# A two-layer hybrid trunk: GpSimd's mixer work to VectorE, gates and branches with tokens on the partitions, and a new ordering clock

## The chip, the cores and the metric

One core of one Trainium2 chip runs the whole forward pass. The metric is the device time of one execution in microseconds (us), as the median of several runs. Four compute engines matter: TensorE (PE in the profile; PEld is its weight load), VectorE (DVE), ScalarE (ACT) and GpSimd (POOL). SyncE (SP) issues the weight transfers.

## The reference, cut to what matters

The input has 256 tokens of 1024 features; there are two layers. Each layer is a feed-forward block, a mixer with three branches that share one input projection, and another feed-forward block.

```
x = x + 0.5 * swiglu_ffn(rms_norm(x, ffn1_norm[l]), ...)
h = rms_norm(x, mix_norm[l])
rg_x, rg_g, sb_q, sb_k, sb_v, c_q, c_kv, k_r, gate_logits = split(h @ w_in[l])
u   = causal_depthwise_conv(rg_x, conv_w[l], conv_b[l])        # 4 taps
y_a = rg_lru(u, ...) * gelu(rg_g)                              # linear recurrence over tokens
y_b = stick_breaking_attention(sb_q, sb_k, sb_v)               # 8 heads of 128
y_c = mla_branch(c_q, c_kv, k_r, ...)                          # latent attention, rope, softmax
g_a, g_b, g_c = split(sigmoid(gate_logits))
merged = g_a * (y_a @ w_branch_a) + g_b * (y_b @ w_branch_b) + g_c * (y_c @ w_branch_c)
x = x + merged @ w_out[l]
x = x + 0.5 * swiglu_ffn(rms_norm(x, ffn2_norm[l]), ...)
```

The output is `rms_norm(x, final_norm)`, all in float32.

## The kernel before, in words

**Arithmetic.** A float32 matmul is made of three in the shorter type float32r. A weight piece (128 partitions by 1024 columns) comes by DMA into `raw`; ScalarE rounds it to `hi` and VectorE subtracts, `lo = raw - hi` (`split_to`, lines 414 to 428). Activations are split alike into a tile `r` (`hilo`, line 461). `AHEAD` lets the split of a piece be issued two pieces before TensorE uses it; `hi` and `lo` have four buffers each.

**Two forms of group.** `feature_group` (line 511) makes 256 output features for all tokens: weights are the stationary operand, features lie on the partitions, and per block of 128 by 128 weights it issues one matmul of 512 columns (`hi` against activation high and low parts) and one of 256 (`lo` against the high part). The two column halves of the bank must then be added, by a ScalarE copy and a VectorE addition (`features`, line 580). `token_group` (line 552) makes 512 features for 2 x 128 tokens: activations are stationary, tokens lie on the partitions, and there are three matmuls of 512 columns per block of 128 tokens by 128 inputs. Its result needs no addition.

**Order.** `MIX_ORDER` (line 31) is the order of a mixer's groups, written by hand: `rgx`, `rgg` (recurrent branch), `q`, `k`, `v` (stick-breaking), `cq`, `ckv`, `uq`, `uqr`, `ukv`, `uv` (latent attention), gates `ga`, `gb`, `gc`, branch projections `bra`, `brb`, `brc`, and `out`. Groups of the trunk go into two large PSUM banks `acc`; short ones (`uq`, `ukv`, the last of a stage) into two of four small banks `side`, which the branches' own small matmuls use too. `small_banks` (line 489) makes the program order run ahead with side work until two are free.

**Side work.** Branch chains are generators. Every recorded operation has an estimated cost (class `Op`), and `Clock` keeps a time for each engine. After each weight block `tasks.tick()` issues what `fits` allows (line 266): a side matmul only if its inputs are at most 60 ns late by that clock. All recorded operations carry line 201 in the profile, so they are told apart by tile names. Each engine runs its own list strictly in order.

**GpSimd** has the first tap of the convolution (line 847), two operations of gelu (865, 866), three products of the recurrent chain (910, 925, 934), half of the query rope (1073), and small norm work.

**Gates and branches.** `gate` (line 1243) evacuates, scales by the token norm (a VectorE product) and takes a tanh. `branch` (line 1256) adds the halves, multiplies by the gate and adds to `merged`; the last one splits the sum for `out`.

Of the kernel before, what the change touches and what calls it, by code (L numbers as in the profile page):

```python
# [14 lines left out]
NT = S // 128  # L15
# [16 lines left out]
v0 k0 rgx0 rgx1 k1 q0 q1 cq0 q2 q3 k2 rgx2 v1 k3 rgx3 rgg0 rgg1 rgg2 rgg3  # L32
gb0 uq0 gb1 uq1 gb2 uq2 gb3 uq3 uqr0 brb0 brb1 ckv0 brb2 brb3 ga0 ukv0 ga1 ukv1 uv0 ga2 ukv2
ga3 ukv3 bra0 bra1 uv1 gc0 bra2 gc1 gc2 gc3 brc0 brc1 brc2 brc3 bra3 out0 out1 out2 out3
# [5 lines left out]
    "ga": ("in", C_G, KD), "gb": ("in", C_G + 1024, KD), "gc": ("in", C_G + 2048, KD),  # L40
    "uq": ("uq", 0, 2), "ukv": ("ukv", 0, 2), "bra": ("bra", 0, KD), "brb": ("brb", 0, KD), "brc": ("brc", 0, KD), "out": ("out", 0, KD),
    "dn1": ("dn1", 0, KF), "dn2": ("dn2", 0, KF),
}
TOKENS = {"last": ("dn2", 0, KF), "v": ("in", 4096, KD), "uqr": ("uq", 1024, 2), "uv": ("ukv", 1024, 2)}


def group_stream(what, n):

    if what == "ckv":
        for k in range(0, 9, 3):  # L50
            yield ("ckv0", "in", k, C_C + 256)
            yield ("ckv1", "in", k, C_C + 256)
    elif what in TOKENS:
# [106 lines left out]
class Op:  # L160


    def __init__(self, engine, name, op, args, kw):
        self.f, self.e, self.args, self.kw = getattr(engine, op), name, args, kw
        self.engine = engine
        out = kw.get("out", args[0] if args else None)
        n = 1
        for d in out.shape[1:]:
            n *= d
        outs = [out] + ([kw["accum_out"]] if kw.get("accum_out") is not None else [])  # L170
        aps = [x for x in (*args, *kw.values()) if hasattr(x, "tensor")]
        self.outs = {x.tensor.name for x in outs}
        self.ins = {x.tensor.name for x in aps if all(x is not o for o in outs)}
        self.table, self.tail = None, 80
        if op == "dma_start":
            self.cost, self.tail = 50, 2500
        elif name == "pe":
            self.tail = 165
            wide = op == "matmul" and args[2].dtype == F32
            self.cost = 2.5 + 0.4167 * (4 * n if wide else max(n, 256))  # L180
        elif name == "act":
            self.table = TABLES.get(kw.get("func"))
            extra = sum(90 for k in ("scale", "bias") if not isinstance(kw.get(k, 0.0), (int, float)))
            self.cost = 95 + extra + 0.833 * n
        elif name == "dve":
            fast = op in ("tensor_scalar", "tensor_copy") and all(x.space != bass.MemoryType.PSUM for x in aps)
            rate = {"reciprocal": 6.5, "tensor_tensor_scan": 2.1}.get(op, 0.55 if fast else 1.042)
            self.cost = 68 + rate * n
        else:
            self.cost = 150 + (166 if kw.get("op") == ALU.pow else 2.1) * n  # L190

# [30 lines left out]
class Tasks:  # L222
# [3 lines left out]

    LIMIT = 1800
# [38 lines left out]
    def fits(self, op, t):  # L266
# [4 lines left out]
        if op.e == "pe":  # L271
            if s > c.t["pe"] + 60:
                return False
# [64 lines left out]
def trunk(tc, xT_in, pos_in, w_in, rgw_in, fin_in, const_in, out):  # L338
# [4 lines left out]
    with ctx:  # L343
# [167 lines left out]
        def feature_group(kts, evac, last=0):  # L511
# [19 lines left out]
            return finish(evac, a, tasks.LAST if last else None)  # L531

# [299 lines left out]
        def rg_x(mx, p):  # L832
            def conv(f):
# [5 lines left out]
                for j in range(2):  # L839
# [7 lines left out]
                    gp.tensor_scalar(us, fs, cw(3), vec[:, vo + V_CB + k:vo + V_CB + k + 1], op0=ALU.mult, op1=ALU.add)  # L847
# [12 lines left out]
        def rg_g(mx, p):  # L860
            def gelu(x):
# [17 lines left out]
        def rg_chain(mx, ps):  # L879
# [3 lines left out]
            for p in ps:  # L883
# [26 lines left out]
                gp.tensor_tensor(I, I, u, op=ALU.mult)  # L910
# [14 lines left out]
                gp.tensor_tensor(I, I, T, op=ALU.mult)  # L925
# [8 lines left out]
                gp.tensor_tensor(g, g, T, op=ALU.mult)  # L934
# [127 lines left out]
        def q_rope(mx):  # L1062
# [128 lines left out]
        def mix(nm, ntasks, nxt, l):  # L1191
# [51 lines left out]
            def gate(b, n):  # L1243
                def sigmoid(f):

                    act.activation(out=f, in_=f, func=AF.Tanh, scale=0.5)
                    yield
                    sig[b, n] = f

                def run(a):  # L1250
                    f = yield from scaled(a, mx["nm"], "rb")
                    yield
                    tasks.spawn(sigmoid(f))
                return run

            def branch(i, b, n):

                def run(a):
                    f = yield from FT.take()
                    hl = (yield from RT.take()) if i == 2 else None  # L1260
                    while (b, n) not in sig or (i and n not in merged):
                        yield 1
                    s = sig.pop((b, n))
                    m = merged[n] if i else None
                    for c, ap in parts(a):
                        fc, sc = two(f)[:, c], two(s)[:, c]
                        act.copy(fc, ap[:, :, 256:512])
                        dve.tensor_tensor(fc, ap[:, :, 0:256], fc, op=ALU.add)
                        if type(a) is not list:
                            yield  # L1270
                            give_banks(a)
                        dve.scalar_tensor_tensor(out=fc, in0=sc, scalar=1.0, in1=fc, op0=ALU.add, op1=ALU.mult)
                        if i:
                            mc = two(m)[:, c]
                            dve.tensor_tensor(mc, mc, fc, op=ALU.add)
                        if i == 2:
                            act.copy(hl[:, c, 0], mc)
                            dve.tensor_tensor(hl[:, c, 1], mc, hl[:, c, 0].bitcast(F32), op=ALU.subtract)
                    yield
                    if type(a) is list:  # L1280
                        give_banks(a)
                    FT.give(s)
                    if i == 0:
                        merged[n] = f
                        return
                    FT.give(f)
                    if i == 2:
                        FT.give(m)
                        mT[n] = hl
# [17 lines left out]
            for g in MIX_ORDER:  # L1307
# [21 lines left out]
                elif what in ys:  # L1329
                    mtask[n] = feature_group(Pairs(mx[ys[what]], lambda p: work[what][p:p + 1] if what == "bra" else work[what], KD), branch(turn[g], what[2], n), last=4 if g == branches[-1] else 0)  # L1330
                elif what == "out":
                    out_tasks.append(feature_group(Pairs(mT, lambda p: [mtask[p]], KD), lambda a, n=n: update_x(n, a, 0.5, nxt), last=4 if n == 3 else 0))
                else:
                    feature_group(kts, gate(what[1], n))
                if what in ys and n == 3:
# [182 lines left out]
```

## Time and profile before

| what | us |
|---|---|
| runs of the kernel | 1460.66, 1460.79, 1461.21 (median 1460.79) |
| the profiled execution | 1463.23 |
| its span (first to last instruction) | 1461.4 |
| TensorE busy | 1442.5 (99% of the span) |
| VectorE busy | 1108.8 (76%) |
| ScalarE busy | 888.8 (61%) |
| GpSimd busy | 144.5 (10%) |

A busy share here is the time in which an engine has at least one instruction in flight. Matmuls overlap, so a busy TensorE can still start its matmuls later than its own pace; the timeline's start times show that, the busy share does not. 1.83 us of the profiled execution lie outside its span.

### The profile page before, as it was taken

The page shows a single profiled execution, that of the slowest core. Times are in us where ns is not written, and L with a number is a line of the kernel's source. Part 1 is how long each engine was busy: PE and PEld are TensorE (multiplying, and loading weights), DVE is VectorE, ACT ScalarE, POOL GpSimd, SP SyncE. Part 2 cuts the span into 40 slices and gives each one's busy share as a digit, 9 for nine tenths or more (in the row PEclk, how much of TensorE's full clock was granted, in tenths as well). Part 3 has the DMA queues.
Part 4 walks back from the last instruction along what each step waited for, and adds up shares of the span by engine and source line. Part 5 has one row for each costly group of instructions (what it writes and reads, how often), then busy time and mean ns, then how long its engine had stood idle before and what let it go on. Part 6 is the DMA issues. An engine that isn't in the chain of part 4 may idle for free.

```text
span 1461.4 us, 20833 instructions
## 1 busy us (share of the span) xinstructions
PE 1442.5 (99%) x8276; PEld 1261.0 (86%) x8276; DVE 1108.8 (76%) x1548; ACT 888.8 (61%) x1365; POOL 144.5 (10%) x118
## 2 busy tenths in 40 slices
PE   8999999999999999999999999999999999999998
PEld 7888889888888888888888888898888888888886
DVE  5887567689987788876677776676989877877853
ACT  4665446888665556555455554479885656566543
POOL 2000001123410000000000000111323000100001
PEclk9999999999999999999999999999999999999999
DMA  6555554444543455455545455544444434545452
GB/s 244 201 185 192 200 179 163 170 151 147 197 148 145 171 179 194 179 200 178 198 173 201 177 198 184 200 159 155 141 171 174 173 138 166 199 175 201 176 199 87
DMA packets 37506, 258.17 MB, mean 177 GB/s; under 512 B 4256, under 2 KB 4640, under 8 KB 6816
## 3 DMA queue, kind: packets, MB, share of 16 engines
q1 hardware_dynamic: 35856, 253.16, 48.0%
q0 software_dynamic: 832, 2.62, 0.6%
q8 instruction: 65, 1.06, 0.3%
q10 hardware_dynamic: 720, 1.05, 0.2%
q14 instruction: 33, 0.27, 0.1%
HBM read 255.77 MB, written 1.05 MB: 176 GB/s over the span
## 4 chain that ended last, share of the span: by engine, by line
PE 90%; DVE 7%; issue 1%; ACT 1%; DMA 0%; ACTq 0%; POOLq 0%; POOL 0%; DVEq 0%
PE acc L201 76%; PE side L201 14%; DVE f L201 3%; DVE lo L201 3%; DVE r L201 1%; DMA x<-xT 0%; ACT f L201 0%; ACT hi L201 0%; ACT r L201 0%; ACTq L396 0%; POOLq L1514 0%; POOL rms L201 0%; DVE rms L201 0%; DVEq L201 0%
## 5 line engine op out<-in xcount | busy, mean ns | idle before, releaser
L201 PE MATMUL acc<-r,hi 128*128 128x512 f32 x3116 | 1000.3, 402 | 0.0
L201 DVE TENSOR_TENSOR lo<-raw,hi 128x1024 fp32r<-128x1024 f32 (+1 forms) x478 | 591.4, 1239 | 231.4 <-ACT hi L201 230.2
L201 PEld LDWEIGHTS acc<-r,lo 128*128 128x128 f32 x3116 | 585.2, 188 | 137.7
L201 PE MATMUL acc<-r,lo 128*128 128x256 f32 x3116 | 613.4, 278 | 0.0
L201 ACT CAST hi<-raw 128x1024 fp32r<-128x1024 f32 (+1 forms) x478 | 496.9, 1045 | 128.8 <-PE acc L201 91.9
L201 PEld LDWEIGHTS acc<-r,hi 128*128 128x128 f32 x3116 | 481.5, 189 | 5.0
L201 POOL TENSOR_TENSOR f<-f,f 128x512 f32<-128x512 f32 (+1 forms) x51 | 90.9, 1787 | 1043.3 <-ACT f L201 959.9
L201 ACT COPY f<-acc 128x512 f32<-128x512 f32 x164 | 96.0, 585 | 121.4 <-PE acc L201 121.2
L201 ACT ACTIVATE f<-f 128x256 f32<-128x256 f32 (+3 forms) x190 | 94.9, 502 | 85.6 <-DVE f L201 84.4
L201 DVE TENSOR_TENSOR f<-acc,f 128x512 f32<-128x512 f32 x166 | 113.9, 686 | 41.6 <-ACT f L201 41.2
L201 DVE TENSOR_TENSOR f<-f,f 128x512 f32<-128x512 f32 (+1 forms) x177 | 125.0, 706 | 7.8 <-ACT f L201 1.6
L201 ACT CAST r<-f 128x256 fp32r<-128x256 f32 (+2 forms) x130 | 58.7, 456 | 63.4 <-DVE f L201 59.7
L201 PE MATMUL acc<-hi,r 128*128 128x512 f32 (+2 forms) x344 | 96.9, 358 | 0.0
L201 PE MATMUL side<-r,hi 128*128 128x512 f32 x260 | 84.5, 396 | 0.0
L201 PE MATMUL side<-f,f 128*128 128x256 f32 (+1 forms) x320 | 71.7, 328 | 0.0
L201 PEld LDWEIGHTS acc<-hi,r 128*128 128x128 f32 x344 | 61.6, 189 | 8.3
L201 DVE TENSOR_TENSOR r<-f,r 128x256 fp32r<-128x256 f32 (+2 forms) x130 | 64.7, 502 | 1.9 <-ACT r L201 1.9
L201 PE MATMUL acc<-lo,r 128*128 128x512 f32 (+2 forms) x172 | 61.0, 355 | 0.0
L201 PE MATMUL side<-r,lo 128*128 128x256 f32 x260 | 60.5, 279 | 0.0
L201 PEld LDWEIGHTS side<-r,hi 128*128 128x128 f32 x260 | 45.6, 188 | 7.5
L201 PEld LDWEIGHTS side<-r,lo 128*128 128x128 f32 x260 | 47.0, 188 | 4.0
L201 PEld LDWEIGHTS side<-f,f 128*128 128x128 f32 x320 | 46.0, 191 | 0.5
(95 smaller groups left out, 839.1 us busy)
## 6 DMA issues: line engine op xcount, KB each, us to landing
raw<-w SPq DMA_DIRECT2D x239, 1024.0 KB, 4.8
f<-rgw POOLq DMA_DIRECT2D x8, 256.0 KB, 3.6
raw<-w SPq DMA_DIRECT2D x4, 256.0 KB, 5.7
out<-f SPq DMA_DIRECT2D x4, 256.0 KB, 2.2
x<-xT ACTq DMA_DIRECT2D x3, 256.0 KB, 6.9
f<-fin POOLq DMA_DIRECT2D x2, 256.0 KB, 3.4
cst<-const SPq DMA_DIRECT2D x1, 336.0 KB, 8.3
x<-xT ACTq DMA_DIRECT2D x2, 128.0 KB, 3.8
```

Of the source, the lines that this page charges most:

```text
L201: return self.f(*self.args, **self.kw)
```

## The change

1. **GpSimd to VectorE:** convolution tap, gelu (its two operations become one), the three products of the recurrent chain and the whole query rope.
2. **Tokens on the partitions:** the six groups of gates and of branch projections become token groups of 512 features (`n` is 0 or 1). The gate's norm scale is then one number per partition, which ScalarE applies in the evacuation. A branch multiplies straight out of PSUM. `merged` now has tokens on the partitions, and is turned back by 16 transposes per layer before `out`.
3. **`out0` and `out1`** are computed together (`feature_pair`): both over the first half of `merged`, then both over the second.
4. **The clock:** matmul costs by new formulas, and a side matmul is issued only if its inputs from other engines were written 300 ns (`LATE`) before TensorE's time.
5. **`MIX_ORDER`** is new.

```diff
-v0 k0 rgx0 rgx1 k1 q0 q1 cq0 q2 q3 k2 rgx2 v1 k3 rgx3 rgg0 rgg1 rgg2 rgg3
-gb0 uq0 gb1 uq1 gb2 uq2 gb3 uq3 uqr0 brb0 brb1 ckv0 brb2 brb3 ga0 ukv0 ga1 ukv1 uv0 ga2 ukv2
-ga3 ukv3 bra0 bra1 uv1 gc0 bra2 gc1 gc2 gc3 brc0 brc1 brc2 brc3 bra3 out0 out1 out2 out3
+v0 k0 rgx0 rgx1 k1 q0 q1 cq0 q2 q3 k2 rgx2 v1 k3 rgx3 rgg0 rgg1 uq0 rgg2 uq1 rgg3 uq2
+gb0 uq3 gb1 uqr0 brb0 ckv0 brb1 ukv0 ga0 ukv1 uv0 ga1 ukv2 bra0 ukv3 uv1 gc0 gc1 bra1 brc0 brc1
+outs0 out2 out3
...
-            wide = op == "matmul" and args[2].dtype == F32
-            self.cost = 2.5 + 0.4167 * (4 * n if wide else max(n, 256))
+            self.cost = self.streamed(op, args[2].dtype if op == "matmul" else F32, n)
...
+    def streamed(op, dtype, n):
+        if op == "transpose":
+            return max(109, 0.852 * n)
+        if dtype == F32:
+            return 2 * max(112, 0.852 * n)
+        if dtype == F32R:
+            return 13.5 + 0.4167 * max(n, 256)
+        return 30 + 0.4167 * n
...
-            if s > c.t["pe"] + 60:
+            if s > c.t["pe"] + 60 or op.settled(c) + self.LATE > c.t["pe"]:
                 return False
...
-                gp.tensor_scalar(t, t, 0.044715, 1.0, op0=ALU.mult, op1=ALU.add)
-                gp.tensor_tensor(t, t, x, op=ALU.mult)
-                act.activation(out=t, in_=t, func=AF.Tanh, scale=0.7978845608028654)
+                dve.scalar_tensor_tensor(out=t, in0=t, scalar=1.0 / 0.044715, in1=x, op0=ALU.add, op1=ALU.mult)
+                act.activation(out=t, in_=t, func=AF.Tanh, scale=0.7978845608028654 * 0.044715)
...
-                gp.tensor_tensor(I, I, u, op=ALU.mult)
+                dve.tensor_tensor(I, I, u, op=ALU.mult)
...
-                    rope((gp, dve)[t], split_heads(f, 8), split_heads(qs[t], 8), split_heads(tmp, 8), 8, t)
+                    rope(dve, split_heads(f, 8), split_heads(qs[t], 8), split_heads(tmp, 8), 8, t)
...
             def gate(b, n):
...
-                    f = yield from scaled(a, mx["nm"], "rb")
+                    fs = []
+                    for t in range(NT):
+                        f = yield from FT.take()
+                        act.activation(out=f, in_=bank_of(a, t), func=AF.Copy, scale=mx["rcol"][t])
+                        fs.append(f)
...
             def branch(i, b, n):
...
+                    for t, f in enumerate(fs):
+                        dve.scalar_tensor_tensor(out=f, in0=f, scalar=1.0, in1=bank_of(a, t), op0=ALU.add, op1=ALU.mult)
+                        if i:
+                            dve.tensor_tensor(merged[n][t], merged[n][t], f, op=ALU.add)
...
+                        for q in range(2):
+                            x = yield from transpose_pair(merged[n], q * 256)
+                            hl = yield from RT.take()
+                            hilo(x, hl)
```

**How the order moves.** Three places are shown. The first is TensorE in the change, at the end of group `rgg1` (bank `acc1`) and the start of `uq0` (banks `side3` and `side0`). The rows between belong to a pair of stick-breaking heads: `tri_r` is the cumulative sum over keys, `f24` and `f21` are the attention weights.

```order
L222 MATMUL acc1_85<-r2_92,hi_2816 128x512 x2
L222 MATMUL acc1_85<-r2_92,lo_2817 128x256 x2
L222 MATMUL side3_89<-r11_101,tri_r_75 128x384 x2
L222 MATMUL side3_89<-f5_111,cst_72 128x128
L222 MATMUL side0_86<-r10_100,tri_r_75 128x384 x2
L222 MATMUL side0_86<-f7_113,cst_72 128x128
L222 MATMUL side1_87<-f24_130,f12_118 128x256
L222 MATMUL side1_87<-f24_130,f13_119 128x128
L222 MATMUL side1_87<-f21_127,f12_118 128x256
L222 MATMUL side1_87<-f21_127,f13_119 128x128
L222 MATMUL side3_89<-r12_102,hi_2864 128x512
```

In the kernel before, `uq0` came after `rgg3` and `gb0`, where no such pair was open; there its first rows stand among matmuls of the recurrent chain:

```order
L201 MATMUL acc0_84<-r2_92,hi_2979 128x512 x2
L201 MATMUL acc0_84<-r2_92,lo_2980 128x256 x2
L201 MATMUL side1_87<-r3_93,r13_103 128x256 x4
L201 MATMUL side0_86<-r11_101,hi_3029 128x512
L201 MATMUL side3_89<-r11_101,hi_3029 128x512
L201 MATMUL side0_86<-r11_101,lo_3030 128x256
L201 MATMUL side3_89<-r11_101,lo_3030 128x256
```

So in the change eight side matmuls of one pair stand together between two groups, where before one row of side work stood. The second place is VectorE in the change at the same point of the program, and then ScalarE. `f28` and `f19` are the evacuations of `rgg0` and `rgg1`, `f7` and `r10` lead to the second `tri_r` above, `r8` is the pair's split output.

```order
L222 TENSOR_TENSOR lo_2888<-raw_2703,hi_2887 128x1024
L222 TENSOR_TENSOR f19_125<-acc1_85,f19_125 128x512
L222 TENSOR_TENSOR f19_125<-f19_125,f2_108 128x512
L222 SCALAR_TENSOR_TENSOR f7_113<-side0_86,f21_127 128x384
L222 TENSOR_TENSOR r10_100<-f7_113,r10_100 128x384
L222 TENSOR_TENSOR r8_98<-side1_87,r8_98 128x2x256
L222 TENSOR_TENSOR lo_2933<-raw_2775,hi_2932 128x1024
L222 TENSOR_TENSOR f4_110<-side3_89,f4_110 128x256
```

On VectorE the addition `f19` and one of the recurrent chain (`f2`) stand ahead of the pair's `f7`, `r10` and `r8`. ScalarE in the change, at the same point of the program:

```order
L222 COPY f19_125<-acc1_85 128x512
L222 ACTIVATE f27_133<-f28_134 128x512
L222 CAST r10_100<-f7_113 128x384
L222 ACTIVATE f24_130<-side3_89 128x384
L222 ACTIVATE f21_127<-side0_86 128x384
L222 CAST r8_98<-side1_87 128x2x256
L222 CAST hi_2932<-raw_2775 128x1024
```

On both engines the rows that lead to `r10` stand behind the evacuation `f19` of `rgg1`. The third place is TensorE in the change inside `outs0`: the transposes of the second half of `merged` (`f24`, `f21` here) and the first matmuls on their split, `r8`.

```order
L222 MATMUL acc1_85<-r14_104,hi_4395 128x512 x2
L222 MATMUL acc1_85<-r14_104,lo_4396 128x256 x2
L222 MATMUL side0_86<-cst_72,f21_127 128x128
L222 MATMUL side0_86<-cst_72,f24_130 128x128
L222 MATMUL side0_86<-cst_72,f21_127 128x128
L222 MATMUL side1_87<-cst_72,f24_130 128x128
L222 MATMUL side1_87<-cst_72,f21_127 128x128
L222 MATMUL side1_87<-cst_72,f24_130 128x128
L222 MATMUL side1_87<-cst_72,f21_127 128x128
L222 MATMUL acc0_84<-r8_98,hi_4432 128x512 x2
```

Seven transposes stand directly ahead of the matmuls that read their result; before, `out0` had none there.

## Rows read from the trace of the kernel before

**Rows 1.** The page's first part: busy time and share of the span, by engine.
```profile
PE 1442.5 (99%) x8276; PEld 1261.0 (86%) x8276; DVE 1108.8 (76%) x1548; ACT 888.8 (61%) x1365; POOL 144.5 (10%) x118
```

**Rows 2.** Windows, one stretch of the first mixer: us, busy us of each engine, clock, DMA.
```profile
320.00:411.00 91.00, 87.46 (x516) 77.12 (x515) 85.32 (x114) 67.62 (x110) 35.75 (x26) 1.00 0.46 162
```

**Rows 3.** Timeline of TensorE, up projection: start us, us, what; feature groups.
```profile
99.87 0.62 PE L201 MATMUL acc<-r,hi 128*128 128x512 f32 x2
...
110.32 0.63 PE L201 MATMUL acc<-r,hi 128*128 128x512 f32 x2
```

**Rows 4.** Timeline of TensorE, a token group (`v0`).
```profile
199.23 0.39 PE L201 MATMUL acc<-lo,r 128*128 128x512 f32 x1
...
205.35 0.39 PE L201 MATMUL acc<-lo,r 128*128 128x512 f32 x1
```

**Rows 5.** Timeline of TensorE: three of a set of four transposes, and the next matmul.
```profile
395.17 0.55 PE L201 MATMUL side<-cst,f 128*128 128x128 f32 x3 [0.16 <-DVE f L201]
395.48 0.70 PE L201 MATMUL acc<-r,hi 128*128 128x512 f32 x2
```

**Rows 6.** Timeline of TensorE in the first mixer, recurrent branch; in brackets idle time, releaser.
```profile
335.23 0.36 PE L201 MATMUL side<-r,r 128*128 128x256 f32 x1
336.47 0.39 PE L201 MATMUL side<-r,r 128*128 128x256 f32 x1 [0.88 <-DVE r L201]
338.57 0.28 PE L201 MATMUL side<-r,r 128*128 128x256 f32 x1
340.31 0.62 PE L201 MATMUL side<-r,r 128*128 128x256 f32 x3 [1.46 <-DVE r L201]
```

**Rows 7.** Timeline of TensorE in the first mixer, latent of keys and values.
```profile
402.29 0.40 PE L201 MATMUL acc<-r,lo 128*128 128x256 f32 x2
403.73 0.70 PE L201 MATMUL side<-f,cst 128*128 128x256 f32 x2 [1.04 <-DVE f L201]
```

**Rows 8.** Groups by line and form: count, busy us, mean ns, idle before.
```profile
L201 ACT COPY f<-acc 128x512 f32<-128x512 f32 x164 | 96.0, 585 | 121.4 <-PE acc L201 121.2
L201 DVE TENSOR_TENSOR f<-acc,f 128x512 f32<-128x512 f32 x166 | 113.9, 686 | 41.6 <-ACT f L201 41.2
L201 DVE TENSOR_TENSOR f<-f,f 128x512 f32<-128x512 f32 x169 | 121.6, 720 | 7.7 <-ACT f L201 1.6
L201 DVE SCALAR_TENSOR_TENSOR f<-side,f 128x384 f32<-128x384 f32 x16 | 8.7, 547 | 0.0
L201 ACT CAST r<-f 128x384 fp32r<-128x384 f32 x16 | 8.0, 513 | 1.4 <-DVE f L201 1.4
L201 DVE TENSOR_TENSOR r<-f,r 128x384 fp32r<-128x384 f32 x16 | 9.5, 602 | 0.0
L201 ACT ACTIVATE f<-side 128x384 f32<-128x384 f32 x32 | 15.7, 490 | 8.6 <-PE side L201 8.0
L201 ACT CAST r<-side 128x512 fp32r<-128x512 f32 x16 | 9.4, 586 | 17.3 <-PE side L201 17.2
L201 DVE TENSOR_TENSOR r<-side,r 128x512 fp32r<-128x512 f32 x16 | 10.9, 683 | 5.1 <-ACT r L201 5.1
```

**Rows 9.** Timeline of ScalarE in the first mixer.
```profile
325.58 0.51 ACT L201 CAST r<-f 128x384 fp32r<-128x384 f32 x1 [0.71 <-DVE f L201]
326.11 1.28 ACT L136 ACT_TABLE_LOAD   x1
327.40 0.64 ACT L201 ACTIVATE f<-f 128x512 f32<-128x512 f32 x1
327.94 1.04 ACT L201 CAST hi<-raw 128x1024 fp32r<-128x1024 f32 x1
```

**Rows 10.** VectorE's `lo`, first in 743 to 903, then in 320 to 411: ns min/median/max.
```profile
L201 DVE TENSOR_TENSOR lo<-raw,hi x58: 1215/1224/1227, 744.7 to 900.2; 128x1024 fp32r<-128x1024 f32 x58
L201 DVE TENSOR_TENSOR lo<-raw,hi x29: 1207/1224/2332, 322.3 to 410.1; 128x1024 fp32r<-128x1024 f32 x29
```

More of the change, by code (lines that the diff above doesn't have):

```diff
@@ L52, in group_stream @@
             yield ("ckv1", "in", k, C_C + 256)
+    elif what == "outs":
+        for h in range(2):
+            for n in range(2):
+                for k in range(KD // 2 * h, KD // 2 * (h + 1), 2):
+                    yield ("two", "out", k, 256 * n)
     elif what in TOKENS:
@@ L190, in __init__, with settled @@
             self.cost = 150 + (166 if kw.get("op") == ALU.pow else 2.1) * n
+    @staticmethod
+    def streamed(op, dtype, n):
[6 more added lines that the diff above has]
+        return 30 + 0.4167 * n
+    def settled(self, c):
+        return max((c.written[n][0] for n in self.ins if n in c.written and c.written[n][1] != self.e), default=0.0)
     def when(self, c, after=0.0):
@@ L222 @@
 class Tasks:
+    LATE = 300
     LIMIT = 1800
@@ L531, in feature_group, with feature_pair @@
             return finish(evac, a, tasks.LAST if last else None)
+        def feature_pair(kts, evacs):
+            nk = len(kts)
+            a = [bank() for _ in range(2)]
+            it = iter(kts)
+            for f in range(2):
+                half = [next(it) for _ in range(nk // 2)]
+                for n in range(2):
+                    for i, (h, _, hl) in enumerate(half, f * nk // 2):
+                        if i % 2 == 0:
+                            wh, wl = next_sub()
+                        cs_ = [slice((i % 2) * 256 + b * 128, (i % 2) * 256 + (b + 1) * 128) for b in range(2)]
+                        for b, c in enumerate(cs_):
+                            pe.matmul(a[n][:, b], wh[:, c], hl, start=i == 0, stop=False, skip_group_check=True)
+                        for b, c in enumerate(cs_):
+                            pe.matmul(a[n][:, b, 0:256], wl[:, c], h, start=False, stop=i == nk - 1, skip_group_check=True)
+                        tasks.tick()
+            return [finish(e, x) for e, x in zip(evacs, a)]
         def plain_group(c, xg, evac, norm):
@@ L1258, in run @@
                 def run(a):
-                    f = yield from FT.take()
-                    hl = (yield from RT.take()) if i == 2 else None
                     while (b, n) not in sig or (i and n not in merged):
                         yield 1
[L1263 to L1269, printed above, removed]
-                            yield
[L1271 to L1278, printed above, removed]
@@ new lines, in run @@
+                    yield
+                    give_banks(a)
+                    if i == 0:
+                        merged[n] = fs
+                        return
+                    FT.give(*fs)
+                    if i == 2:
+                        for q in range(2):
+                            x = yield from transpose_pair(merged[n], q * 256)
+                            hl = yield from RT.take()
+                            hilo(x, hl)
+                            yield
+                            side.give(x)
+                            mT[2 * n + q] = hl
+                        FT.give(*merged[n])
@@ L1329, in mix @@
                 elif what in ys:
-                    mtask[n] = feature_group(Pairs(mx[ys[what]], lambda p: work[what][p:p + 1] if what == "bra" else work[what], KD), branch(turn[g], what[2], n), last=4 if g == branches[-1] else 0)
+                    mtask[n] = token_group(Pairs(mx[ys[what]], lambda p: work[what][p:p + 1] if what == "bra" else work[what], KD), branch(turn[g], what[2], n), last=4 if g == branches[-1] else 0)
+                elif what == "outs":
+                    out_tasks += feature_pair(Pairs(mT, lambda p: [mtask[p // 2]], KD), [lambda a, n=n: update_x(n, a, 0.5, nxt) for n in range(2)])
                 elif what == "out":
-                    out_tasks.append(feature_group(Pairs(mT, lambda p: [mtask[p]], KD), lambda a, n=n: update_x(n, a, 0.5, nxt), last=4 if n == 3 else 0))
+                    out_tasks.append(feature_group(Pairs(mT, lambda p: [mtask[p // 2]], KD), lambda a, n=n: update_x(n, a, 0.5, nxt), last=4 if n == 3 else 0))
                 else:
-                    feature_group(kts, gate(what[1], n))
-                if what in ys and n == 3:
+                    token_group(kts, gate(what[1], n))
+                if what in ys and n == 1:
                     RT.give(*mx[ys[what]].values())
```

36 lines of the change are left out of this document (15 added, 21 removed).

## Prediction, made before the change was run

> **What bounds the kernel now.** I read the busy table first: TensorE is busy for 1442.5 of the 1461.4 us of the span, VectorE for 1108.8, ScalarE for 888.8, GpSimd for 144.5 [rows 1]. Work taken from the other three engines is therefore worth something only where TensorE waits for them. The table by windows shows the densest stretch of the first mixer: from 320 to 411 us VectorE is busy for 85.32 of 91 us and TensorE for 87.46, at a granted clock of 1.00 [rows 2]. There VectorE could matter. A busy share does not show a late start, because matmuls overlap, so I read the starts in the timeline. A pair of a feature group's matmuls (512 and 256 columns) takes (110.32 - 99.87) / 30 = 0.348 us [rows 3]; three matmuls of 512 columns in a token group take 3 x (205.35 - 199.23) / 27 = 0.68 us [rows 4]. Against such paces I looked for starts that come late. In a mixer three stand out: two `r` products of the recurrent chain, where 1.24 and 1.74 us lie between two starts whose pace is 0.12 us, so 1.12 and 1.62 us are lost, both released by VectorE [rows 6]; and the latent of keys and values, where 1.44 us lie between two starts whose pace is 0.23, so 1.21 us are lost [rows 7]. That is 3.95 us per layer. The rest of TensorE's time is its own work, so what counts is the number of its matmuls, and the waits that the new order makes.
>
> **The change part by part.**
>
> *Tokens on the partitions.* Twelve matrices of 1024 by 1024 (three gates and three branches in two layers) change their form. As features, one is 64 pairs, 64 x 0.348 = 22.29 us [rows 3]. As tokens, it is 96 matmuls of 512 columns at 0.2267, 21.76 us [rows 4]. Twelve times the difference is -6.3 us. The order counts bear this out: 1536 feature matmuls fewer, 1152 token matmuls more. Added are 32 transposes of `merged`, each a start apart from the next by (395.48 - 395.17) / 3 = 0.103 us [rows 5], together +3.3 us. **Net -3.0 us.**
>
> *Evacuations.* 46 ScalarE copies of 585 ns and 46 VectorE additions of 686 ns go [rows 8]; 24 scaled ScalarE evacuations and 24 VectorE products out of PSUM come. TensorE does not wait for any of these before, so I cost the difference at nothing. The cover is TensorE's own work; without it the engines would still be lighter.
>
> *GpSimd's work on VectorE.* Thirty-two products of 128 by 512 leave GpSimd, with 8 other steps of gelu, 16 conv taps and 12 rope operations. On VectorE the form f<-f,f rises only from 169 to 171 instructions, because the gates' and branches' products leave it; in all VectorE goes from 1550 to 1530. GpSimd's load falls from 123 to 55. VectorE's weight differences `lo` have the same median beside GpSimd work as without (1224 ns), but there the longest took 2332 ns against 1227 [rows 10]; TensorE was not late for `lo` anywhere before, so I count nothing for this. The chain whose `r` was late by 1.12 and 1.62 us [rows 6] is shorter by GpSimd's hand-overs, and the margin of 300 ns asks for inputs that are written. I take both waits, and that of [rows 7], as **gone: -3.95 x 2 = -7.9 us**.
>
> *`uq0` between `rgg1` and `rgg2`.* `small_banks` makes the program issue side work until two small banks are free. In the changed order that pulls eight side matmuls of a stick-breaking pair in between, and on ScalarE and VectorE their inputs stand behind the evacuation of `rgg1`. From the end of `rgg1` the chain is, by the groups' means: copy 0.585, addition 0.686, then about 0.6 of the following `f2` product before the next starts (0.72 for its whole), `f7` 0.547, `r10` on ScalarE 0.513 and on VectorE 0.602 [rows 8]; then the sum over keys on TensorE with some 0.5, the exponential 0.490 [rows 8] and the product with the values, some 0.35; both are estimates from 384 and 3 x 256 columns at the pace of [rows 4]. Together about 5.4 us with hand-overs. TensorE has about 1.6 us of work of its own beside it (eight side matmuls). **+3.8 us per layer.** The ends: 3.0 if the chain starts with `f2` overlapped and hand-overs cost nothing, 4.5 if each step pays another 0.1 us, which is what ScalarE's overlap of consecutive operations shows [rows 9].
>
> *`outs0`.* Seven transposes stand directly ahead of the matmuls on their split. From the last one a ScalarE rounding of 586 ns and a VectorE difference of 683 ns [rows 8] and about 0.4 us of hand-overs, 1.7 us, lie before the next matmul that needs both; 0.55 us of that is covered by transposes. **+1.1 us per layer**, between 0.5 and 1.5.
>
> *Other small banks.* Three later places in the new order ask for a small bank or an input within a microsecond of its last reader: `uq2` (0.45), the latent ahead of `ukv0` (0.6) and `uv1` behind the evacuation of `bra0` (0.8). The trace of before has no such row; between nothing and 1.85 us per layer I take the middle, **+0.9**.
>
> *Sum.* -3.0 - 7.9 + 2 x (3.8 + 1.1 + 0.9) = +0.7 us. On the profiled execution, 1463.23, that is 1463.9. The median of the runs is 1460.79, and 2.4 us lower; by the same difference the changed kernel's median is **1461.5**. About 0.2% (2.9 us) is what a measurement can tell from no change, so I forecast no difference. With the bounds of the new waits alone this case runs from 1457 to 1465.
>
> **The rivals.**
>
> *Faster: the new waits are small.* If the chain behind `rgg1` takes its low end of 3.0, and the other small banks are free in time, the sum is -10.9 + 2 x (3.0 + 1.1) = -2.7; with `outs0` covered as well it is -4.9, that is 1455.9. For it speaks that the margin of 300 ns and 68 fewer GpSimd operations make the rest of the side work arrive earlier, and that the trace before has few late starts outside [rows 6, 7]. Against it, the rows behind `f19` are in strict order on both engines, and no margin applies where `small_banks` forces the issue.
>
> *Slower: ScalarE's weight roundings come late.* Between `rgg0` and `gb1` the change's order has nine table loads on ScalarE where the stretch of [rows 2] had four. One takes 1.28 us [rows 9], so five more are 6.4 us on an engine that was busy for 67.62 of 91 us [rows 2]. Its idle time is mostly waiting for a side bank in order, and so can't all be used. Weights are rounded two pieces ahead, and a piece of eight blocks lasts 8 x 0.348 = 2.8 us [rows 3], so TensorE loses time once a lead of 5.6 us is used up. Then between 0.8 us (6.4 less 5.6) and all of 6.4 us per layer is lost: 3.6 us in the middle, and 1461.5 + 7.2 = 1468.7. It decides from the point where `hi` is the last input of a weight matmul to arrive. Against it: in the window ScalarE had 23.4 us idle, and the feature evacuations of gates in that stretch are replaced by fewer operations.
>
> Here a rule and a row differ. The next activation starts 1.29 us after the load does, and the one before it ends as the load starts: nothing is lost around it [rows 9]. The Trainium skill, "ScalarE: Activation LUTs", section "What ACT_TABLE_LOAD costs", gives about 1283 ns for the load and some 1380 ns for a drain, 2.66 us for each switch of set. The load agrees with the trace, the drain doesn't. By that rule (an estimate from that page) five more loads would cost 13.3 us per layer, 7.7 beyond the lead, and the kernel would take about 1477 us. Since the row shows no such drain, I give that case 2 in 100.
>
> *Slower: the change doesn't remove the waits.* The recurrent chain keeps its length on the two other engines, and VectorE now does all of it. If the waits of [rows 6, 7] only move to other rows, 7.9 us come back: 1461.5 + 7.9 = 1469.4. For it: VectorE is busy for 85.32 of 91 us there [rows 2], and GpSimd's 35.75 us are of work that in part goes to it. Against it: at the new place the chain runs beside weight matmuls until the margin is met.
>
> **How the numbers follow.** I give my forecast 0.42, the faster rival 0.28, late roundings 0.17, waits that move 0.11 and the table loads' drain 0.02. The predicted time is the likeliest, 1461.5. The range reaches from a little below the faster rival's 1455.9 (the low end of `outs0`, 2 x 0.6, and rounding) to just past 1469.4: 1454 to 1470. Faster by over 0.2% is below 1457.9, 0.28; within it 0.42; slower, above 1463.7, 0.30.
>
> **What would show it.** In the changed profile, TensorE's timeline should show a stretch of about 5 us between `rgg1`'s last matmul and `uq0`'s first, with idle time released by ScalarE and VectorE in turn; a start about 1 us late at the first matmul on `r` in `out0`; and no row like those of [rows 6, 7]. Starts of token groups in gates and branches should be 0.227 us apart, and 384 matmuls be missing. The faster rival shows a stretch of 4.5 us or less behind `rgg1`; late roundings show as starts of `acc<-hi,r` matmuls released by ScalarE's `hi` between `rgg0` and `gb1`; waits that move as `side<-r,r` rows with over 1 us idle, released by VectorE. I would be wrong altogether if TensorE's pace in token groups of gates were not that of `v0`, by 12 x 96 x 0.01 = 11.5 us for each 0.01 us.

## The result, and the profile after

The changed kernel takes 1475.22 us (median of 4 runs, 1474.57 to 1475.75), the one before 1461.0 us on the same chip: ratio 1.0096, interval 1.0078 to 1.0113. The kernel is slower by 14 us where no difference was forecast, and lies outside the range of 1454 to 1470.

The first part of its page answers to [rows 1]. TensorE's busy time hardly grows, and every other engine is less busy: VectorE by 47.7 us, ScalarE by 11.2, GpSimd by 101.

```profile
PE 1447.9 (98%) x7924; PEld 1247.4 (85%) x7924; DVE 1061.1 (72%) x1528; ACT 877.6 (60%) x1341; POOL 43.4 (3%) x50
```

A first answer comes from the starts of the same weight piece in both timelines of TensorE: from its first matmul in `v0` to a first matmul in the next feed-forward block. I call that stretch a **mixer** below; it leaves out what happens at the start of the program, and in most kernels here the two mixers differ by 0.2 us or less. Before, the mixers last 566.29 - 203.77 = 362.52 us and 362.68; in the change, 570.79 - 201.44 = 369.35 and 369.27. That is twice 6.7 us, 13.4 of the 14.2 us lost. The feed-forward blocks last the same to within 0.1 us. (The two profiled executions differ by only 11.0 us, since the one before reached its first split weight piece 2.3 us later, at 25.1 us of its span against 22.8.)

The place is the first one of the prediction. TensorE in the change at the end of `rgg1` and the start of `uq0`, in the timeline:

```profile
323.02 0.40 PE L222 MATMUL acc<-r,lo 128*128 128x256 f32 x2
323.25 0.51 PE L222 MATMUL side<-r,tri_r 128*128 128x384 f32 x2
323.60 0.38 PE L222 MATMUL side<-f,cst 128*128 128x128 f32 x2
327.46 1.28 PE L222 MATMUL side<-r,tri_r 128*128 128x384 f32 x2 [3.49 <-ACT r L222]
328.55 0.63 PE L222 MATMUL side<-f,cst 128*128 128x128 f32 x2
328.97 2.44 PE L222 MATMUL side<-f,f 128*128 128x256 f32 x8
331.16 0.71 PE L222 MATMUL side<-r,hi 128*128 128x512 f32 x2
```

The reader sees 7.9 us between the first side matmul (323.25) and `uq0` (331.16), for the eight rows of side work of the order above, which are 16 instructions in the trace. From 323.71 (the last start before the stop; its row groups two) to 327.46 TensorE starts nothing. The chain that it waits for, on ScalarE and then on VectorE:

```profile
323.62 0.58 ACT L222 COPY f<-acc 128x512 f32<-128x512 f32 x1
324.10 0.64 ACT L222 ACTIVATE f<-f 128x512 f32<-128x512 f32 x1
326.90 0.51 ACT L222 CAST r<-f 128x384 fp32r<-128x384 f32 x1 [2.17 <-DVE f L222]
```
```profile
323.86 1.22 DVE L222 TENSOR_TENSOR lo<-raw,hi 128x1024 fp32r<-128x1024 f32 x1
324.99 0.68 DVE L222 TENSOR_TENSOR f<-acc,f 128x512 f32<-128x512 f32 x1
325.71 0.69 DVE L222 TENSOR_TENSOR f<-f,f 128x512 f32<-128x512 f32 x1
326.32 0.55 DVE L222 SCALAR_TENSOR_TENSOR f<-side,f 128x384 f32<-128x384 f32 x1
327.44 0.56 DVE L222 TENSOR_TENSOR r<-f,r 128x384 fp32r<-128x384 f32 x1 [0.58 <-ACT r L222]
```

It is the chain of the prediction, row by row: copy, a weight difference that keeps VectorE until 325.0, addition, product `f2`, `f7`, `r10`. What the prediction does not have stands in the table by windows of the change, in the column after POOL's, the granted clock:

```profile
324.00:327.00 3.00, 0.00 (x0) 0.00 (x0) 2.83 (x4) 0.83 (x3) 0.00 (x0) 1.00 0.25 49
327.00:331.00 4.00, 3.54 (x10) 2.94 (x11) 0.56 (x1) 1.29 (x3) 0.00 (x0) 0.57 0.53 225
331.00:334.00 3.00, 3.00 (x19) 2.62 (x18) 1.68 (x2) 2.56 (x5) 0.00 (x0) 1.00 0.02 5
```

After the stop the clock falls to 0.57 in the mean of four microseconds (0.50 is the lower of its two levels, 1.2 GHz), and the side matmuls that `uq0` waits for run slowly: eight of them take 2.44 us, against 1.72 at a clock of 1.00 in e6 below.

Five more late starts of TensorE in the first mixer of the change, in order: at `uq2`, at the latent of [rows 7], at `ukv0`, at `uv1`, and behind the transposes of `outs0`:

```profile
346.90 0.47 PE L222 MATMUL side<-r,hi 128*128 128x512 f32 x1 [0.24 <-DVE f L222]
...
402.88 0.70 PE L222 MATMUL side<-f,cst 128*128 128x256 f32 x2 [1.64 <-DVE f L222]
...
407.80 0.50 PE L222 MATMUL side<-r,hi 128*128 128x512 f32 x1 [0.22 <-ACT f L222]
...
457.10 0.50 PE L222 MATMUL side<-hi,r 128*128 128x512 f32 x1 [0.49 <-DVE r L222]
...
535.66 0.72 PE L222 MATMUL acc<-r,hi 128*128 128x512 f32 x2 [0.96 <-DVE r L222]
```

Against the usual pace these starts are late by 0.40, 1.80, 0.46, 0.84 and 1.21 us. The late `r` products of [rows 6] are gone.

### The profile page after: what moved, and what is told of

Read it like the earlier page. It is cut to its first block, busy times and chain, and to the rows that moved or that the text cites. A ratio compares the mean times of both kernels' runs of the same rounds, so it can differ in the third digit from the quotient of the medians.

```text
span 1472.4 us, 19989 instructions
## 1 busy us (share of the span) xinstructions
PE 1447.9 (98%) x7924; PEld 1247.4 (85%) x7924; DVE 1061.1 (72%) x1528; ACT 877.6 (60%) x1341; POOL 43.4 (3%) x50
## 3 DMA queue, kind: packets, MB, share of 16 engines
q10 hardware_dynamic: 720, 1.05, 0.2%
HBM read 255.77 MB, written 1.05 MB: 174 GB/s over the span
## 4 chain that ended last, share of the span: by engine, by line
PE 83%; ACT 9%; DVE 5%; issue 2%; DMA 0%; POOL 0%; POOLq 0%; SPq 0%; ACTq 0%
PE acc L222 69%; PE side L222 14%; ACT f L222 4%; DVE f L222 3%; ACT hi L222 2%; ACT L143 2%; DVE lo L222 1%; DVE r L222 1%; ACT r L222 1%; DMA raw<-w 0%; POOL rc L222 0%; POOLq L1554 0%; POOL rms L222 0%; SPq L419 0%; DVE rms L222 0%
## 5 line engine op out<-in xcount | busy, mean ns | idle before, releaser
L222 PE MATMUL acc<-r,hi 128*128 128x512 f32 x2380 | 756.1, 399 | 1.9 <-DVE r L222 1.9
L222 PEld LDWEIGHTS acc<-r,lo 128*128 128x128 f32 x2380 | 447.1, 188 | 105.5
L222 PE MATMUL acc<-r,lo 128*128 128x256 f32 x2380 | 468.0, 278 | 0.0
L222 PEld LDWEIGHTS acc<-r,hi 128*128 128x128 f32 x2380 | 364.5, 189 | 4.4 <-DVE r L222 2.8
L222 PE MATMUL acc<-hi,r 128*128 128x512 f32 (+2 forms) x1048 | 341.7, 392 | 0.0
L222 PEld LDWEIGHTS acc<-hi,r 128*128 128x128 f32 x1048 | 194.3, 188 | 35.1
L222 PE MATMUL acc<-lo,r 128*128 128x512 f32 (+2 forms) x524 | 198.5, 379 | 0.0
L222 PEld LDWEIGHTS acc<-lo,r 128*128 128x128 f32 x524 | 98.7, 188 | 16.3
L222 DVE TENSOR_TENSOR f<-acc,f 128x512 f32<-128x512 f32 x120 | 82.1, 685 | 16.5 <-ACT f L222 16.4
L222 PE MATMUL side<-hi,r 128*128 128x512 f32 x200 | 64.4, 394 | 1.0 <-DVE r L222 1.0
```

Source lines behind the costliest of these rows:

```text
L222: return self.f(*self.args, **self.kw)
```

## The experiments

All times are against the kernel before on the same chip. The mixer durations are worked out from each trace as above.

| kernel | median us | ratio to before, interval | mixers, us |
|---|---|---|---|
| before | 1461 to 1463 | | 362.5, 362.7 |
| the change | 1475.22 | 1.0096, 1.0078 to 1.0113 | 369.4, 369.3 |
| e1 uq0 behind rgg3 | 1458.74 | 0.9976, 0.9967 to 0.9986 | 361.5, 361.5 |
| e2 stop half filled | 1475.34 | 1.0084, 1.0070 to 1.0098 | 368.3, 369.4 |
| e3 no margin | 1476.09 | 1.0094, 1.0080 to 1.0108 | 369.3, 369.3 |
| e4 GpSimd's work back | 1474.95 | 1.0082, 1.0070 to 1.0095 | 369.6, 370.2 |
| e5 e1 and e4 | 1475.87 | 1.0098, 1.0084 to 1.0111 | 369.4, 370.1 |
| e6 stop filled | 1471.89 (one run) | | 368.3, 368.3 |
| e7 e1, old clock | 1473.30 | 1.0080, 1.0067 to 1.0092 | 368.8, 369.0 |
| e8 before with part 1 | 1472.09 | 1.0073, 1.0061 to 1.0086 | 368.7, 368.7 |
| e9 uq0 in a large bank | 1464.73 | 1.0019, 1.0010 to 1.0029 | 365.0, 365.0 |
| e10 e1, uv1 later | 1460.20 | 0.9991, 0.9982 to 1.0000 | 362.0, 362.0 |
| e11 e1, no margin | 1460.47 (one run) | | 361.4, 361.4 |
| e12 e5, old clock | 1469.31 | 1.0051, 1.0037 to 1.0065 | 366.7, 366.7 |

**e1: `uq0` behind `rgg3`.**

```diff
-rgg0 rgg1 uq0 rgg2 uq1 rgg3 uq2
-gb0 uq3 gb1 uqr0 brb0 ckv0 ...
+rgg0 rgg1 rgg2 rgg3 uq0
+gb0 uq1 gb1 uq2 brb0 uq3 uqr0 ckv0 ...
```

The groups `uq1` to `uq3` and `uqr0` move back with it.

> Edit: uq0 stands after rgg3 instead of between rgg1 and rgg2 (uq1, uq2, uq3 one place later each), all else as in the changed kernel. Theory (the loss is the stop behind rgg1: 3.65 us of late start and then some 2 us of half clock, per layer): both go, 2 x 5.7 = 11.4 us, so 1475.2 - 11.4 = 1463.8, give or take 2; no window at a clock under 1.00 in the mixer. Rival (VectorE's or ScalarE's load is the cause, the place only shows it): the wait moves to another row and the time stays within 3 us of 1475.2.

The kernel becomes faster than both. Its timeline of TensorE shows the two `tri_r` pairs of the same pair of heads apart, each between weight matmuls, and none of them late; the clock in the window that was low is 1.00:

```profile
327.89 0.51 PE L222 MATMUL side<-r,tri_r 128*128 128x384 f32 x2
...
328.37 0.71 PE L222 MATMUL acc<-r,hi 128*128 128x512 f32 x2
...
329.86 0.52 PE L222 MATMUL side<-r,tri_r 128*128 128x384 f32 x2
```
```profile
327.00:331.00 4.00, 4.00 (x26) 3.65 (x25) 4.00 (x8) 3.68 (x7) 0.00 (x0) 1.00 0.70 244
```

A mixer loses 7.8 us, not 5.7: in the same step the late start at the latent of keys and values (1.80 us in the change) went, and the two small ones at `uq2` and `ukv0` (0.40 and 0.46). With the 3.65 and 0.42 us of the two `r10` starts and 1.05 us for the clock (e6) that makes 7.8. Moving a group deals the order of what follows anew. The theory holds, its price was low by 2 us per layer.

**e2 and e6: the stop filled with work.** In `stick_pair`, for the pair that stands in the stop:

```diff
+                if p == 3 and j == 1:
+                    o = yield from side.take()
+                    for i in range(FILL):
+                        pe.matmul(o[:, 0:128], warm, warm, start=True, stop=True)
```

The ordering clock counts these matmuls at nothing, so that all other work keeps its order.

> Edit: 30 small bf16 matmuls on zeros (128 columns) into the pair's still unused output bank, at the place of the stop behind rgg1, in both layers; the order of all other instructions stays. It adds work that is thrown away. Theory (the granted clock falls because TensorE stands still for 3.5 us): the chain on ScalarE and VectorE is as long as before, but TensorE is busy and the clock stays at 1.00 from 327 to 331 us, so 2 x about 2.1 us come back: 1471. Rival (the slow matmuls after the stop have another cause, their operands or banks): 1475.2 or a little more, the clock low as before.

> Edit: 58 instead of 30 small matmuls in the stop behind rgg1; 30 of them took 1.84 us and left 1.82 us of idle time. Theory (the clock falls because TensorE has nothing to do for some microseconds): with the stop filled to within 0.2 us the clock is 1.00 in both layers, and each mixer lasts about 1.1 us less than the 369.3 of the changed kernel, 368.2. Rival: the clock falls in at least one layer as before.

With 30 matmuls the fill lasted 1.84 us, and 1.82 us of idle time stayed behind it. In the first layer the clock held, in the second it fell, though the instructions are the same. The windows of e2, first layer, then second:

```profile
328.00:330.00 2.00, 0.66 (x2) 0.41 (x3) 1.15 (x3) 0.90 (x2) 0.00 (x0) 1.00 0.83 307
330.00:332.00 2.00, 2.00 (x12) 1.72 (x12) 0.00 (x0) 0.49 (x1) 0.00 (x0) 1.00 0.43 180
...
1054.00:1056.00 2.00, 0.71 (x2) 0.31 (x2) 1.24 (x3) 0.90 (x2) 0.00 (x0) 0.86 0.78 274
1056.00:1058.00 2.00, 2.00 (x7) 1.82 (x8) 0.00 (x0) 0.49 (x1) 0.00 (x0) 0.50 0.51 213
```

The first mixer was shorter by 1.1 us, the second was not; so e2 alone was inconclusive. With 58 matmuls (e6) the clock is 1.00 in both layers and both mixers are shorter by 1.0 us than in the change. TensorE in e6:

```profile
322.62 0.51 PE L223 MATMUL side<-r,tri_r 128*128 128x384 f32 x2
...
323.18 3.40 PE L223 MATMUL side<-warm 128*128 128x128 bf16 x58
326.85 0.44 PE L223 MATMUL side<-r,tri_r 128*128 128x384 f32 x1 [0.26 <-ACT r L223]
327.44 0.44 PE L223 MATMUL side<-r,tri_r 128*128 128x384 f32 x1 [0.15 <-DVE r L223]
...
327.94 1.72 PE L223 MATMUL side<-f,f 128*128 128x256 f32 x8
329.42 0.71 PE L223 MATMUL side<-r,hi 128*128 128x512 f32 x2
```

So the fall of the clock is a consequence of the standstill, and costs about 1.05 us per layer (1.10 and 0.96); I had put it at 2.1. The standstill itself is not shortened by any filling: the chain on the other engines is as long as before.

**e3 and e11: no margin.**

```diff
-            if s > c.t["pe"] + 60 or op.settled(c) + self.LATE > c.t["pe"]:
+            if s > c.t["pe"] + 60:
```

> Edit: the margin of 300 ns is taken out of the rule (60 ns late is allowed again), new matmul durations kept. Theory: the margin has no part in the loss; the stop behind rgg1 is forced by the banks and stands: 1475 within 2 us. Rival (the margin makes side work late and so the small new waits): 3 to 6 us faster, about 1470, with the stop still there.

> Edit: uq0 behind rgg3, new matmul costs, margin of 300 ns taken out. Theory (of the new clock, the costs moved the stop and the margin does nothing): mixers as with uq0 moved alone, 361.5 within 0.3 us. Rival (the margin did it): a stop at uq0 as with the old clock, mixers near 368.9.

The margin changes nothing that can be seen: 369.3 with and without it in the change, 361.4 and 361.5 with `uq0` moved.

**e4 and e5: GpSimd's work back on GpSimd**, in the change and with `uq0` moved. The diff is that of part 1, turned round.

> Edit: GpSimd's work goes back to GpSimd (tap, gelu, three products, half of the rope), all else as in the changed kernel. Theory (this part of the change only removed the two waits of the recurrent chain): those waits come back in part and the stop behind rgg1 stays: 1475 to 1481. Rival (the load on VectorE makes the chain behind rgg1 long): the stop shrinks by the f2 product and more, and the kernel is 3 us or more faster than 1475.2.

> Edit: uq0 behind rgg3 as in the run before, and GpSimd's work back on GpSimd. Theory (moving that work to VectorE is by itself a gain, since it removes late r products of the recurrent chain; the loss was the place of uq0): 2 to 4 us per layer slower than with uq0 moved alone, 1463 to 1467, with starts of r products late by 1 us and more, released by products that follow GpSimd. Rival (VectorE's load is what hurts): as fast or faster than 1458.7.

In e4 the stop behind `rgg1` is gone: `uq0` starts directly behind it. So part 1 did take part in it, which my theory had denied. But other waits come in its place, one of them of the kind of [rows 6], and the sum is 0.3 to 1.0 us per layer worse. In e4 and e5, the latest rows of TensorE are:

```profile
354.82 0.50 PE L222 MATMUL side<-r,r 128*128 128x256 f32 x2 [2.38 <-DVE r L222]
```
```profile
332.75 0.44 PE L222 MATMUL side<-r,tri_r 128*128 128x384 f32 x1 [1.98 <-DVE r L222]
...
393.30 0.33 PE L222 MATMUL side<-cst,f 128*128 128x128 f32 x1 [2.13 <-POOL f L222]
```

e5 against e1 is what part 1 is worth where the order suits it: 7.9 and 8.6 us per mixer, against 2 to 4 expected. Nor did the loss come by the late `r` products that I had named: none is late in e5; a sum over keys waits for VectorE, with the clock at 0.50 behind it, and transposes wait for GpSimd. The rival, that VectorE's load is what hurts, falls for e5; for e4 both were half right.

**e7 and e12: the old clock**, with `uq0` moved, and the same with GpSimd's work back.

```diff
-            self.cost = self.streamed(op, args[2].dtype if op == "matmul" else F32, n)
+            wide = op == "matmul" and args[2].dtype == F32
+            self.cost = 2.5 + 0.4167 * (4 * n if wide else max(n, 256))
```

(and the margin out, as in e3)

> Edit: uq0 behind rgg3, and the old clock (old matmul costs, no margin). Theory (the clock's new numbers make issue times truer, and are a small gain or none once the order is right): within 3 us of 1458.7, rather above. Rival (the clock is what put the waits at the latents, 0.6 and 0.3 us per layer, and others): 2 us or more faster than 1458.7.

> Edit: token groups, transposes, out0 with out1 and uq0 behind rgg3; GpSimd's work on GpSimd, old clock: the change's parts 2 and 3 without 1 and 4. Theory (each part deals the order anew, and a stop comes where a demand for two small banks meets an open pair): with nothing tuned to it, waits of 5 us and more per layer, mixers of 365 to 371. Rival (the token form itself is the gain, the others don't matter): own work 1.5 us per layer less than before and the old waits, mixers near 361 to 363.

I expected e7 within 3 us of e1; its mixers are 7.3 and 7.5 us longer. Its trace shows the very stop of the change, now at the place to which `uq0` had been moved:

```profile
336.71 1.28 PE L223 MATMUL side<-r,tri_r 128*128 128x384 f32 x2 [3.23 <-ACT r L223]
337.79 0.63 PE L223 MATMUL side<-f,cst 128*128 128x128 f32 x2
338.21 2.53 PE L223 MATMUL side<-f,f 128*128 128x256 f32 x8
340.49 0.71 PE L223 MATMUL side<-r,hi 128*128 128x512 f32 x2
```

Since e11 shows that the margin does nothing, it is the matmul costs. That by the old ones the pair's second half was held back until `uq0` demanded the banks is my reading of the order of the rows, not tried by itself. In e12 there is no such stop, but the two waits of the kernel before stand there again, to the same length as [rows 6], and, in the first layer, four of 0.8 to 1.9 us at the latents, `uv1` and `outs0`. The mixers, 366.7 us, lie where the theory put them, but by these waits and not by a stop:

```profile
334.41 0.39 PE L223 MATMUL side<-r,r 128*128 128x256 f32 x1 [0.88 <-DVE r L223]
...
338.25 0.63 PE L223 MATMUL side<-r,r 128*128 128x256 f32 x3 [1.45 <-DVE r L223]
```

**e8: part 1 alone in the kernel before** (the diff of part 1).

> Edit: the kernel before with part 1 of the change alone (GpSimd's work on VectorE). Theory: the two late r products (1.12 and 1.62 us per layer) go, the rest stays: 1461 - 5.5 = 1455.5. Rival (VectorE, busy for 94% of the stretch from 320 to 411 us, becomes the bound): waits of the same size or larger in that stretch, 1461 or slower.

The rival's outcome, by two mechanisms. The late `r` products of [rows 6] are gone, as I expected, and the wait of [rows 7] as well. In their place a stop of the same kind stands ahead of `uq0`, which in that kernel follows `gb0`: the two `tri_r` starts are late by 0.7 and 1.7 us, and the clock falls behind them. Windows of e8:

```profile
342.00:344.00 2.00, 0.57 (x2) 0.32 (x3) 1.66 (x3) 0.22 (x1) 0.00 (x0) 1.00 0.96 393
344.00:346.00 2.00, 2.00 (x9) 1.73 (x9) 0.00 (x0) 0.49 (x1) 0.00 (x0) 0.55 0.18 74
...
444.00:446.00 2.00, 0.00 (x0) 0.00 (x0) 1.89 (x6) 1.66 (x5) 0.00 (x0) 1.00 0.00 0
446.00:448.00 2.00, 1.78 (x7) 1.65 (x8) 1.39 (x2) 0.37 (x1) 0.00 (x0) 0.65 0.03 8
```

At this stop the load on VectorE is not the bound: VectorE is busy for 1.66 of the two microseconds of the stop and for 0.00 of the next two. The larger part of the loss comes later in the same mixer: two starts at 441 and 446 us are late by 1.8 and 2.8 us, both released by VectorE, and the clock falls once more.

```profile
441.30 0.73 PE L201 MATMUL acc<-r,hi 128*128 128x512 f32 x2 [1.43 <-DVE r L201]
...
446.22 0.91 PE L201 MATMUL acc<-r,hi 128*128 128x512 f32 x2 [2.44 <-DVE r L201]
```

There VectorE is busy for 9.5 of the 10 us before 440 and for 5.5 of the 6 us behind, so the rival's mechanism, VectorE as the bound, is not excluded for these two waits; no run tries it. In all, the same work on another engine cost 6 us per layer in this order.

**e9: `uq0` in a large bank**, in the place that the change gives it.

```diff
-            a = small_banks() if last or nk <= 2 else bank()
+            a = small_banks() if (last or nk <= 2) and not large else bank()
...
-                    feature_group(Latent(0), head_T(mx, "qn", n, "rbq"))
+                    feature_group(Latent(0), head_T(mx, "qn", n, "rbq"), large=n == 0)
```

> Edit: uq0 keeps its place between rgg1 and rgg2, but takes one large bank instead of two small ones, so that nothing forces the open pair's side work there. Theory (the demand for two small banks is what makes the stop, not the place as such): the 3.65 us and the half clock go, and rgg2 waits up to 1 us for the large bank of rgg1; each mixer 364 to 366 instead of 369.3, the kernel near 1467. Rival (the pair is late whatever asks for it): a stop of 3 us and more a little later, mixers of 368 and above.

The stop is gone, and the pair's matmuls stand among those of `rgg2`. The price is a wait for the large bank, 2.1 us rather than 1, released by VectorE, with the clock at 0.50 from 328 to 330 us behind it. The latent of [rows 7], late by 1.80 us in the change, comes without a wait here:

```profile
326.66 0.78 PE L222 MATMUL acc<-r,hi 128*128 128x512 f32 x2 [1.94 <-DVE f L222]
...
400.95 0.59 PE L222 MATMUL side<-f,cst 128*128 128x256 f32 x2
```

The mixers are 365.0 us, as expected. It shows that the demand for two small banks while a pair is open is the cause of the stop, and not the place as such. And it shows more than I asked: `MIX_ORDER` is that of the change, yet the waits at the latent of keys and values, `uq2` and `ukv0` are gone as in e1. In this order they too come with that demand.

**e10: `uv1` behind `gc0`.**

```diff
-bra0 ukv3 uv1 gc0 gc1 bra1 brc0 brc1
+bra0 ukv3 gc0 uv1 gc1 bra1 brc0 brc1
```

> Edit: uq0 behind rgg3, and uv1 one group later (behind gc0), where the evacuation of bra0 no longer stands directly ahead of it. Theory: the late start at uv1, 0.86 us per layer, goes and nothing else moves much: 1458.7 - 1.7 = 1457. Rival (every shift of a group deals the order of the side work anew): another wait of 1 us or more, 1459 or slower.

The wait at `uv1` went, and one of 0.92 us came at the start of a branch product, released by ScalarE; the mixers are 0.5 us longer than in e1. The rival was right in its time. The two waits are nearly equal (0.86 and 0.92 us), so they are not where the 0.5 us lie.

```profile
504.90 0.50 PE L222 MATMUL acc<-hi,r 128*128 128x512 f32 x1 [0.68 <-ACT r L222]
```

## Why the prediction was wrong

- **What bounds the kernel**: right. The loss is all in late starts of TensorE; no other engine became busier.
- **Tokens on the partitions**, -1.5 us per layer: the count and the pace were right (352 instructions fewer in all; token groups of gates start 0.227 us apart in e1), but the gain does not show. Less the late starts named in this section and the clock, a mixer lasts 358.6 us before, in the change and in e1 alike. Starts late by less than 0.25 us each must have used up the 1.5 us; they are not traced to places.
- **The three old waits**, -3.95 per layer: the two of [rows 6] went (-2.74; e8, with part 1 alone, has neither, and in e12, without parts 1 and 4, both stand again). The step "I take both waits, and that of [rows 7], as gone" failed for [rows 7] in this order: that wait stayed, and grew from 1.21 to 1.80 us. That is 1.8 us per layer. In e1, e8 and e9 it is gone, so the work of the change allows it to go; it is the order dealt out after `uq0` that keeps it.
- **`uq0` between `rgg1` and `rgg2`**, +3.8: this is the term that failed by most. The stop was foreseen, and the `r10` products start 3.65 and 0.42 us late, 4.07 together. But the step priced the stop and nothing after it. By e1 the place of `uq0` costs 7.8 us per layer: 4.07 for the stop, 1.05 for the clock that falls after the standstill (e6), and 2.66 for the late starts at the latent of keys and values, `uq2` and `ukv0`, which e9 removes too. That 3.8 and 4.07 agree is in part luck: at a clock of 1.00 the stretch lasts 6.8 us (322.62 to 329.42 in e6) and not 5.4, and TensorE's own rows in it take about 2.7 us (6.8 less 4.07) and not 1.6; the two errors nearly cancel.
- **`outs0`**, +1.1: it is 1.21.
- **Other small banks**, +0.9 as the middle between nothing and 1.85: they are 0.60 and 0.30 at the latent of the queries, 0.40 at `uq2`, 0.46 at `ukv0` and 0.84 at `uv1`, 2.6 together, over the upper bound. I had looked for places that ask for a bank, not for inputs that come late after each re-dealt group.

In the prediction's own terms, measured less forecast, a layer got 1.5 (tokens), 1.8 ([rows 7]), 0.3 (the stop), 1.05 (the clock), 0.1 (`outs0`) and 1.7 us (other small banks) more than the sum had. That is 6.4 us; the sum had +0.35, and +6.7 was measured.

Of the rivals priced from rows, "waits that move" came nearest in its time (1469.4), but not in its place: the change has no late `r` product of the recurrent chain. Late weight roundings did not happen (no weight matmul waited for `hi`), and their premise was too large: a mixer of the change has 17 table loads in its trace against 15 before, two more and not five. Nor did a drain around table loads show: behind 35 of the 37 loads of the change the next activation starts 0.01 us after the load ends. By the Trainium skill ("ScalarE: Activation LUTs", "What ACT_TABLE_LOAD costs"), with the prediction's five loads, the time was estimated as 1477. The measured time is near that figure by accident, since e1 removes the loss with the same 37 table loads.

The deeper mistake is in the sum's form. I priced each wait as if the rest of the order stayed. e1, e4 and e9 against the change, e7 and e10 against e1, e8 against the kernel before, and e5 against e1, are single edits that move a mixer by 0.3 to 8.6 us, and in each the side work's issue is dealt anew after it. The stop stands where `small_banks` meets a pair of heads half done: in the change, e7 and e8, with part 1 present in all three; it does not come in e1, e9, e4 and e12.

What decides is therefore the place and the banks of `uq0` together with the matmul costs. With the new costs, VectorE's share and `uq0` behind `rgg3` (e1), the same change is faster than the kernel before: 1458.74 against 1462.84 us on the same chip. Its mixers are 1.0 and 1.2 us shorter, which is the 2.2 us that the trace can account for. It stays open how the demand of `uq0` brings the wait at the latent of keys and values: e7 has the stop and not this wait, and e12 has this wait in its first layer and no stop.

## What to carry to other kernels

In a kernel whose side work is ordered by a planner, look first for the demands that override the planner (here, a group that asks for two small banks) and ask what can be half done when each is reached; here that place was worth 7.8 us per mixer. Price a wait together with what the engine does after it, since a stop of TensorE of some microseconds can be followed by matmuls at half clock. And judge a change of engine or form only after the order has been set again for it: part 1 cost 6 us per layer in one order (e8 against before) and brought 8 or more in another (e1 against e5).

## What the runs showed of the hardware

- The granted clock of TensorE fell after a single stop of 3.5 us (the change) and of 3.2 us (e7), and after shorter ones not always: after 1.82 us it held in one layer of e2 and fell in the other; after 2.13 us in e5 it held in the first layer (1.00 from 394 to 398 us) and fell in the second (0.57 from 1122 to 1126); after 1.94 us it fell in e9 (0.50 from 328 to 330 us). So the length of one stop does not tell. The Trainium skill ("TensorE: Matmul & The Clock Gate", "Part 1: The HAM clock gate (the "warmup" mystery)") says that a gate lowers this clock by how busy the engine has been lately; that the clock depends on idleness agrees with e6, where only the idle time was taken away.
- Filling matmuls of 128 bf16 columns start 0.056 us apart at a clock of 1.00 (58 last 3.40 us and 30 last 1.84, so (3.40 - 1.84) / 28), and 58 of them filled a stop of 3.5 us to within 0.3.
- The first matmul on a weight piece that is split on the chip starts between 22.2 and 25.1 us after the span's start in the traces here, whichever kernel it is, while the two mixers of a kernel differ by 0.2 us or less in most of them (by 0.6 and 0.7 in e4 and e5, and by 1.1 in e2, where the clock fell in one layer alone). A difference of 2 us between two kernels is better read from the same stretch of both traces than from two totals.
